# Prompt head norm moved to compression's banks, and the low half of w_out emitted ahead of the samples' value stage

## The chip, the cores and the metric

The kernel runs on one core of one Trainium2 chip. The metric is device microseconds of one execution. Before the change it takes 1236.41 us (median of 3 runs, 1235.61 to 1237.87).

## The reference

One inference step of a decoder layer, for a prompt of 512 tokens and for 8 samples of 4 tokens (32 rows), with shared weights of width 1024:

```
h = RMSNorm(x); P = h @ W_in
x += W_out [ headnorm(NSA(P_nsa)) || sigmoid(o) * headnorm(mLSTM(P_mlstm)) ]
x += CrossAttn(RMSNorm(x), memory K/V)
x += SwiGLU(RMSNorm(x))
y = RMSNorm_final(x)
```

NSA is sparse attention with three parts whose gated outputs are added: over compressed blocks (`compress`: a small two-layer network over each 32 rows of keys and of values), over selected blocks of 64 raw rows, and over a window of 512 rows. For the samples the cached rows are gathered from pages, transposed, scored against the queries, put through a softmax and multiplied with the gathered values. `headnorm` is an RMS norm over the 64 values of each head. The change concerns the prompt's NSA head norm, the samples' attention, and the first half of `W_out`.

## The kernel before, in words

All 544 tokens (512 of the prompt, 32 of the samples) lie in columns. The activations `oF` (the mixed heads' outputs) and `xT` (the residual) hold 8 blocks of 128 features by 544 columns. Products with weights are made of three matmuls, since a 32-bit operand is split into a high and a low part: `split` writes the high part on ACT (L213) and the low part on POOL or DVE (L214), and `mm3` issues `hi*hi`, `hi*lo` and `lo*hi` (L218 to L220). Columns are handled in two halves of 272: the low half holds prompt columns only, the high half the other 240 and the 32 samples. The split parts of the low half are the tiles `mh` and `ml`; weight chunks of `w_out` are `wraw`, split to `whi` and `wlo`.

Parts of the kernel are generators that yield between small steps. `weave` runs two of them alternately, `chain` one behind the other with its pace, `drain` runs one to its end. The text order that results gives each instruction a priority; a scheduler then orders the instructions of each engine by what it thinks is ready and by that priority. Each engine runs its own list in order, waiting where an operand or a buffer is not free.

The place in question is the end of the samples' attention, beside the second call of `compress`. Names there:

- `sample()`: for two groups of four samples each, score stage first: `keys` gathers are transposed on PE (L1518, tile `tp`), copied by `evac` (L206 on ACT, L208 on DVE, tile `kt`), multiplied with the queries (L1528, tile `sp`), and the exponentials are taken on ACT (L1701, tile `SS`). Then the value stage: `SS` is transposed (L1518), copied (`PTs`), and multiplied with the gathered values (L1722, tile `po`).
- `evac` puts one copy of every `flip[1]` on DVE and the others on ACT: 1 in 2 at first, 1 in 4 while `flip[1]` is 4.
- `finals_p`: the prompt's NSA outputs. L1398 multiplies the compressed part's probabilities with its values, L1401 adds them into `oF`, L1402 squares, L1407 sums over a head with a matmul against `bones`, L1408 copies back; then a logarithm (L1411), an exponential (L1412) and the scaling (L1415) make the norm.
- PSUM banks: `tp` has two, `sp` one, `po` one; `bd` has two, `xa` and `xc` one each. `bank(p)` takes the next bank of one pool, `rot(...)` the next of several in turn; `pxb` is the pair `xa`, `xc`. Compression uses `bd`, `xa`, `xc` (its lines L1216 to L1246, L1296); so does the projection `w_out`.
- `load_xT(i)` transposes a tile of the input x into `xT` (L1817), in six tiles; `fetch_x` loads those tiles by DMA.
- `early_mix`: splits the low half of `oF` into `mh` and `ml`, and fetches and transposes x. `open_late` and `finals_s` prepare the high half and the samples' final norm; `close_sample` is a last step.

Before the change `finals_p` is called inside `sample()`, behind the value stage of group 0, and `early_mix` is called after `drain(fg)`, that is, behind everything of the samples. Then come the loops over the chunks of `w_out` for the low half and the high half, and behind them the cross attention.

Of the kernel before, what the change touches and what calls it, by code (L numbers as in the profile page):

```python
# [6 lines left out]
F32 = mybir.dt.float32  # L7
# [29 lines left out]
def body(tc, I, O, stage=99, dbg=None):  # L37
    nc = tc.nc
    with ExitStack() as top:
        def pool(name, bufs=1, side="left", stack=None, space=None):  # L40
            kw = dict(name=name, bufs=bufs)
            if space is not None:
                kw["space"] = space
            else:
                kw["side"] = side
                kw["reuse_waits"] = "tile"
            return (stack or top).enter_context(tc.tile_pool(**kw))

        ptp = pool("ptp", 2, space=PSUM)
        psp = pool("psp", 1, space=PSUM)  # L50
        ppo = pool("ppo", 1, space=PSUM)
        pxa = pool("pxa", 1, space=PSUM)
        pxc = pool("pxc", 1, space=PSUM)
        pxb = [pxa, pxc]
        pbd = pool("pbd", 2, space=PSUM)

        def bank(p):
            if p is pxb:
                return rot(pxa, pxc)
            return p.tile([128, 512], F32, name=p_names[id(p)])  # L60
# [4 lines left out]
        def rot(*pools):  # L65
            key = tuple(id(p) for p in pools)
            turn[key] = turn.get(key, -1) + 1
            return bank(pools[turn[key] % len(pools)])
# [6 lines left out]
        right = {}  # L75

        def push(name, **kw):
            st = ExitStack()
            right[name] = st
            return pool(name, stack=st, **kw)  # L80

        def pop(name):
            right.pop(name).close()
# [43 lines left out]
        wp = push("wp", bufs=2, side="left")  # L127
# [182 lines left out]
        def drain(*gens):  # L310
            for g in gens:
                for _ in g:
                    pass
# [248 lines left out]
        p = bank(ptp)  # L562
# [33 lines left out]
        wp = push("wp", bufs=2, side="left")  # L596
# [147 lines left out]
        def need(x):  # L744
            while x not in done:
                yield 1
# [644 lines left out]
        def finals_p(var):  # L1391
            yield from need(("p", 1))
            var = var[:, :2048].rearrange("p (a b n) -> p a b n", a=2, b=2)
            for j in range(5):
                if j < 4:
                    acc = bank(psp)
                    for v in range(2):
                        nc.tensor.matmul(acc[64 * v:64 * v + 64], vcP[32 * j:32 * j + 32, v], PcT[32 * j:32 * j + 32, v],  # L1398
                                         start=True, stop=True)
                    oj = oF[:, j, :512]  # L1400
                    nc.vector.tensor_tensor(oj, oj, acc, op=OP.add)  # L1401
                    nc.scalar.activation(var[:, j // 2, j % 2], oj, AF.Square)  # L1402
                    yield
                if j > 0:
                    p = bank(ptp)
                    vj = var[:, (j - 1) // 2, (j - 1) % 2]
                    nc.tensor.matmul(p, bones, vj, start=True, stop=True)  # L1407
                    nc.scalar.activation(vj, p, AF.Copy)  # L1408
                if j < 4:
                    yield  # L1410
            nc.scalar.activation(var, var, AF.Ln, bias=eps_t)  # L1411
            nc.scalar.activation(var, var, AF.Exp, scale=-0.5)  # L1412
            for j in range(4):
                oj, vj = oF[:, j, :512], var[:, j // 2, j % 2]
                nc.vector.scalar_tensor_tensor(oj, oj, gh[:, j:j + 1], vj, op0=OP.mult, op1=OP.mult)  # L1415
            yield

        def sample():
            yield from need(("w", 1))
            sc = push("sc", side="right")  # L1420
# [120 lines left out]
            for g in range(2):  # L1541
# [29 lines left out]
                p = bank(ptp)  # L1571
# [15 lines left out]
            def half(name, g, hf, qs=range(4), ex=False):  # L1587
                r = []
                for q in qs:
                    t_ = cgs["free"].pop(0) if ex else sc.tile([128, 1024], F32, name="gat", bufs=8)  # L1590
                    gather(t_, name, 4 * g + q, 1 + hf)
                    r.append(t_)
                return r
# [50 lines left out]
            for g in range(2):  # L1644
# [22 lines left out]
                SS = sc.tile([128, 2080], F32, name="SS", bufs=2)  # L1667
# [39 lines left out]
            for g in range(2):  # L1707
                SS, rs = st_[g]
                if g:
                    yield from need("free")  # L1710
                    G[1, "v1"] += half("cache_v_slc", 1, 1, range(2, 4), True)
                PT_ = probs(lambda i: SS[:, 128 * i:128 * i + 128])
                yield
                po_ = bank(ppo)
                for c in range(4):
                    vg = G[g, "v0" if c < 2 else "v1"]
                    if c < 3:
                        PX = probs(lambda i: SS[:, 512 * c + 512 + 128 * i:512 * c + 640 + 128 * i])
                    for i in range(4):
                        ii = 4 * (c % 2) + i  # L1720
                        for q in range(4):
                            nc.tensor.matmul(po_[32 * q:32 * q + 32, 0:128], PT_[:, i, 32 * q:32 * q + 32],  # L1722
                                             vg[q][:, 128 * ii:128 * ii + 128], start=c == 0 and i == 0, stop=False)
                    PT_ = PX
                    if c == 0:
                        p = bank(ptp)
                        nc.tensor.transpose(p[:32, 0:128], SS[:, 2048:2080], ident)
                        PN_ = sc.tile([32, 128], F32, name="PN")
                        nc.vector.tensor_copy(PN_, p[:32, 0:128])
                    if c == 1 and g == 0:  # L1730
                        G[1, "v0"] = half("cache_v_slc", 1, 0)
                    if c == 3 and g == 0:
                        G[1, "v1"] = half("cache_v_slc", 1, 1, range(2))
                    yield
                nc.tensor.matmul(po_[:, 0:128], PN_, kvs[:, 384:512], start=False, stop=True)
                nc.vector.reciprocal(rs[:, 2:3], rs[:, 1:2])
                nc.vector.tensor_tensor(rs[:, 2:3], rs[:, 2:3], g3[:, g, 1:2], op=OP.mult)
                nc.vector.scalar_tensor_tensor(ocs[:, g], po_[:, 0:128], rs[:, 2:3], ocs[:, g], op0=OP.mult, op1=OP.add)
                yield
                if g == 0:  # L1740
                    yield from finals_p(sc.tile([128, 2080], F32, name="SS", bufs=2))
            pop("sc")
            pop("mixS")

# [30 lines left out]
        hot = {}  # L1775
# [22 lines left out]
        def fetch_x(ids, t_):  # L1798
            for i, x in zip(ids, t_):
                t0, n = xtl[i]  # L1800
                xts[i] = x
                nc.sync.dma_start(x[:n], I["x_prompt"][0, t0:t0 + n] if i < 5 else I["x_sample"].rearrange("b t d -> (b t) d"))

        def cgat():
            return cgp.tile([128, 2048], F32, name="cgat", bufs=2)

        def cgat_x():
            t_ = cgat().rearrange("p (i d) -> p i d", i=2)
            return [t_[:, 0], t_[:, 1]]

        def load_xT(i):
            t0, n = xtl[i]
            x = xts[i]
            for c in range(2):
                p = rot(psp, ppo)
                for k in range(4):
                    nc.tensor.transpose(p[:, n * k:n * k + n], x[:n, 512 * c + 128 * k:512 * c + 128 * k + 128], ident[:n, :n])  # L1817
                evac(xT[:, 4 * c:4 * c + 4, t0:t0 + n], p[:, :4 * n].rearrange("p (k t) -> p k t", k=4))

        def close_sample():  # L1820
            load_xT(5)
            yield

        def early_mix():
            hot["wp"] = push("wp", bufs=2, side="right")
            hot[0] = [wt.tile([128, KT, HALF], R32, name=f"m{c}", bufs=1) for c in "hl"]
            for k in (4, 5, 6, 7, 0, 1, 2, 3):
                split(hot[0][0][:, k], hot[0][1][:, k], oF[:, k, :HALF], nc.gpsimd if k % 2 else nc.vector)
            fetch_x((2, 3), cgat_x())
            fetch_x((4, 5), cgat_x())  # L1830
            for i in range(5):
                load_xT(i)

        def front():
# [31 lines left out]
        def wo_chunk(c):  # L1866
            return lambda: load_w([wo[:, 256 * c:256 * c + 256]], KT, fill=wo_fill(c))

        wt = hot["wt"] = push("wt", bufs=2, side="left")
# [4 lines left out]
        won.append((raw1,) + tuple(wt.tile([128, 2048], R32, name=f"w{x}").rearrange("p (k c) -> p k c", k=KT)  # L1874
                                    for x in ("hi", "lo")))
        fetch_x((0, 1), [wt.tile([128, D], F32, name=f"xt{i}", bufs=1) for i in range(2)])
        drain(fg)
        flip[1] = 2
        early_mix()
        hxp, lp, wp = hot["hx"], hot["lp"], hot["wp"]  # L1880
        if stage == 5:
            drain(finals_s())
# [9 lines left out]
        acc = [kct[:, 0, :HALF], acct[:, hs[1]]]  # L1892
# [697 lines left out]
        for hf in (1, 0):  # L2590
            for j in range(8):
                p = rot(*dbk)
# [24 lines left out]
```

## Time and profile before

| | |
|---|---|
| median of 3 runs | 1236.41 us |
| profiled execution | 1243.24 us, of which the span is 1241.5 us |
| mean granted PE clock | 0.974 |
| PE busy | 1174.3 us, 95% |
| DVE busy | 841.2 us, 68% |
| ACT busy | 612.4 us, 49% |
| POOL busy | 558.6 us, 45% |
| PE busy, 530 to 590 us | 48.42 of 60 us |

The profiled execution is 6.83 us longer than the median of the runs; its span leaves out 1.7 us around the program. Times in the text below are microseconds from the span's start. A row of the instructions in order of time gives start, length, engine, line, operation, output and inputs; a square bracket at its end gives the idle time ahead of it and what ended it.

### The profile page before, as it was taken

To read this page: it belongs to the slowest core of one execution; us is meant where nothing else is said; L and a number is where in the kernel's file an instruction comes from. 1 tells how busy PE (TensorE), PEld (TensorE's weight loads), DVE (VectorE), ACT (ScalarE), POOL (GpSimd) and SP (SyncE) were. 2 spreads that over 40 slices of the span, in tenths; PEclk is the share of its full clock that TensorE was granted. 3 is DMA by queue.
4 is the path that set the end of the run, shared out by engine and by line. 5 is a ranking of instruction groups with operands and counts; after the bars stand their busy time and mean duration, and the time that the engine had idled before them with its cause. 6 is when DMAs were issued, how large, how long until landed. Compare 5 with 4: busy or idle time off the path is not lost.

```text
span 1241.5 us, 24581 instructions
## 1 busy us (share of the span) xinstructions
PE 1174.3 (95%) x9220; PEld 1066.7 (86%) x9220; DVE 841.2 (68%) x1901; ACT 612.4 (49%) x1414; POOL 558.6 (45%) x686
## 2 busy tenths in 40 slices
PE   7999999899997989988999989999899999999996
PEld 5998999588885878854999987599899999999996
DVE  6337683567787687653754756554998888888874
ACT  5235665745545444466542423342665565555452
POOL 1013353566666266542342100043885576476342
PEclk9999999899997999999999998999999999999998
DMA  7324240141253185566767298630032333322411
GB/s 232 102 53 105 86 153 1 51 137 44 78 171 115 42 283 176 178 227 205 206 135 171 83 239 288 231 128 2 1 119 86 103 96 107 106 94 77 137 52 73
DMA packets 141769, 154.30 MB, mean 124 GB/s; under 512 B 17449, under 2 KB 123689, under 8 KB 141394
## 3 DMA queue, kind: packets, MB, share of 16 engines
q1 hardware_dynamic: 131922, 119.17, 32.0%
q0 software_dynamic: 9728, 33.56, 8.3%
q8 instruction: 73, 1.20, 0.4%
q14 instruction: 46, 0.38, 0.1%
HBM read 141.67 MB, written 13.12 MB: 125 GB/s over the span
## 4 chain that ended last, share of the span: by engine, by line
PE 49%; DVE 8%; ACT 3%; DMA 2%; issue 2%; SPq 1%; POOL 1%; POOLq 0%; DVEq 0%; ACTq 0%
PE xc L2291 7%; PE xa L2291 7%; PE bd L2291 5%; PE tp L2291 5%; PE bd L220 3%; PE bd L219 3%; PE bd L218 3%; DVE sp L2231 1%; DMA mkv<-in_cache_mem_k 1%; PE xa L1296 1%; PE tp L1518 1%; PE bd L2190 1%; PE xa L218 1%; PE xa L219 1%; PE xa L220 1%
## 5 line engine op out<-in xcount | busy, mean ns | idle before, releaser
L214 POOL TENSOR_TENSOR al<-fraw,ah 128x512 fp32r<-128x512 f32 (+1 forms) x104 | 127.5, 1227 | 152.4 <-ACT ah L213 124.0
L213 ACT ACTIVATE whi<-wraw 128x1024 fp32r<-128x1024 f32 (+3 forms) x74 | 62.5, 890 | 57.5 <-DMA wraw<-in_w_xv 28.2
L214 DVE TENSOR_TENSOR wlo<-wraw,whi 128x1024 fp32r<-128x1024 f32 (+3 forms) x74 | 73.6, 1026 | 19.1 <-ACT whi L213 19.0
L213 ACT ACTIVATE ah<-fraw 128x512 fp32r<-128x512 f32 (+1 forms) x112 | 65.8, 593 | 38.0 <-PE xc L2291 11.8
L218 PE MATMUL bd<-w1h,xh 128*128 128x256 f32 x256 | 82.6, 325 | 0.9 <-issue 0.9
L220 PE MATMUL bd<-w1h,xl 128*128 128x256 f32 x256 | 75.6, 298 | 3.0 <-DVE xl L214 3.0
L1198 POOL TENSOR_TENSOR xs<-xf 128x256 f32<-128x256 f32 x64 | 55.8, 878 | 50.2 <-PE xa L1296 30.5
L219 PE MATMUL bd<-w1l,xh 128*128 128x256 f32 x256 | 75.7, 297 | 0.0
L1296 PE MATMUL xa<-ws,xs 128*128 128x256 f32 x256 | 71.2, 400 | 2.4 <-DVE bq L1470 1.3
L625 POOL TENSOR_SCALAR sb<-sb,rs,gat 128x128 f32<-128x128 f32 (+3 forms) x64 | 46.1, 724 | 54.4 <-DVE rs L624 40.2
L213 ACT ACTIVATE xh<-xf 128x512 fp32r<-128x512 f32 x64 | 40.0, 629 | 45.5 <-DVE xf L1191 20.0
L213 ACT ACTIVATE ah<-sp 128x512 fp32r<-128x512 f32 (+1 forms) x64 | 35.5, 555 | 50.1 <-DVE sp L2231 22.8
L220 PEld LDWEIGHTS bd<-w1h,xl 128*128 128x128 f32 x256 | 48.9, 192 | 6.4 <-DVE xl L214 3.8
L1296 PEld LDWEIGHTS xa<-ws,xs 128*128 128x128 f32 x256 | 46.5, 201 | 8.5 <-issue 2.9
L218 PEld LDWEIGHTS bd<-w1h,xh 128*128 128x128 f32 x256 | 49.1, 193 | 5.0 <-issue 3.9
L214 DVE TENSOR_TENSOR xl<-xf,xh 128x512 fp32r<-128x512 f32 x64 | 47.5, 746 | 8.6 <-ACT xh L213 7.7
L219 PEld LDWEIGHTS bd<-w1l,xh 128*128 128x128 f32 x256 | 49.4, 193 | 4.5 <-issue 2.8
L219 PE MATMUL bd<-hlo,whi 128*128 128x272 f32 x176 | 52.0, 296 | 0.0
L218 PE MATMUL bd<-hhi,whi 128*128 128x272 f32 x176 | 51.7, 294 | 0.0
L1191 DVE STREAM_TRANSPOSE xf<-cgat 128x512 f32<-128x512 f32 x64 | 44.7, 703 | 10.2 <-POOL xs L1198 8.4
L220 PE MATMUL bd<-hhi,wlo 128*128 128x272 f32 x176 | 51.3, 292 | 0.0
L2231 DVE TENSOR_TENSOR sp<-fraw 128x512 f32<-128x512 f32 (+1 forms) x32 | 47.8, 1494 | 0.2
(990 smaller groups left out, 4667.9 us busy)
## 6 DMA issues: line engine op xcount, KB each, us to landing
fraw<-in_w_gate SPq DMA_DIRECT2D x11, 1024.0 KB
fraw<-in_w_up SPq DMA_DIRECT2D x11, 1024.0 KB
fraw<-in_w_down SPq DMA_DIRECT2D x24, 384.0 KB
mkv<-in_cache_mem_k SPq DMA_DIRECT2D x64, 128.0 KB
mkv<-in_cache_mem_v SPq DMA_DIRECT2D x16, 512.0 KB
wraw<-in_w_in SPq DMA_DIRECT2D x8, 512.0 KB
wraw<-in_w_xq SPq DMA_DIRECT2D x4, 1024.0 KB
wraw<-in_w_xk SPq DMA_DIRECT2D x4, 1024.0 KB
```

The source lines that it names most:

```text
L213: nc.scalar.activation(hi, src, AF.Copy)
L214: (eng or nc.gpsimd).tensor_tensor(lo, src, hi, op=OP.subtract)
L218: nc.tensor.matmul(out, ah, bh, start=first, stop=False, **kw)
L219: nc.tensor.matmul(out, ah, bl, start=False, stop=False, **kw)
L220: nc.tensor.matmul(out, al, bh, start=False, stop=last, **kw)
L625: (nc.vector, nc.gpsimd)[1].tensor_scalar(sb[:, :n], sb[:, :n], rs, gat[:, i, 3 * h + 1 + br:3 * h + 2 + br], op0=OP.mult, op1=OP.mult)
L1191: nc.vector.transpose(xf.rearrange("p a (q i) -> p q a i", q=4), gs[0].rearrange("p (q t a i) -> p t q a i", q=4, t=4, a=4)[:, t])
L1198: nc.gpsimd.tensor_tensor(xs_.rearrange("p c (v j) -> p v c j", v=2), xg[:, 0], xg[:, 1], op=OP.add)
L1296: nc.tensor.matmul(dst[2], ops[2][:, kk], w1s[t][2][:, kk], start=t == 0 and kk == 0, stop=t == 3 and kk == 1, skip_group_check=True)
L1518: nc.tensor.transpose(p[:, 128 * i:128 * i + 128], srcs(i), ident)
L2231: nc.vector.tensor_tensor(o, a, b, op=op)
L2291: nc.tensor.matmul(p[:, :HALF], w[a][:, k], x[b_][:, k], start=first and k == 0 and i == 0, stop=last and k == n - 1 and i == 2, skip_grou ...
```

## The change

The norm `finals_p` writes its sums to the banks `bd`, `xa` and `xc` (in place of `sp` and `tp`), takes the tile `ml` of the low half as scratch, and is run by `early_mix`, not by `sample()`. `early_mix` is called ahead of `drain(fg)`, so what remains of the samples' generators comes behind it in the text. x tiles 3 to 5 are loaded and transposed in `close_sample`, and x tiles 0 to 2 use the bank `sp` alone. The buffers `wp` are opened after the drain.

```
 def finals_p(var):
...
-                    acc = bank(psp)
+                    acc = rot(pbd, pxb)
...
-                    p = bank(ptp)
+                    p = rot(pbd, pxb)
...
 def sample():
...
-                if g == 0:
-                    yield from finals_p(sc.tile([128, 2080], F32, name="SS", bufs=2))
...
 def load_xT(i):
...
-                p = rot(psp, ppo)
+                p = bank(psp) if i < 3 else rot(psp, ppo)
...
 def close_sample():
-            load_xT(5)
-            yield
+            yield 6
+            fetch_x((4, 5), cgat_x())
+            for i in range(3, 6):
+                load_xT(i)
+                yield

 def early_mix():
-            hot["wp"] = push("wp", bufs=2, side="right")
+            drain(finals_p(wt.tile([128, 2176], F32, name="ml", bufs=1)))
...
-            fetch_x((4, 5), cgat_x())
-            for i in range(5):
+            for i in range(3):
                 load_xT(i)
...
         fetch_x((0, 1), [...])
+        early_mix()
         drain(fg)
         flip[1] = 2
-        early_mix()
+        hot["wp"] = push("wp", bufs=2, side="right")
```

No instruction of PE is added or taken away; two of `load_xT`'s copies go from DVE to ACT. The order of the engines' lists changes from about 530 us on.

On ACT before, at the start of group 1's value stage (`PTs` are the copies of the transposed probabilities, `SS<-SS` with 2048 columns the norm's logarithm and exponential):

```order
L1408 ACTIVATE SS<-tp 128x512
L1411 ACT_TABLE_LOAD
L1411 ACTIVATE SS<-SS,eps_t 128x2048
L206 ACTIVATE PTs<-tp 128x512 x2
L1412 ACT_TABLE_LOAD
L1412 ACTIVATE SS<-SS 128x2048
L206 ACTIVATE PTs<-tp 128x512
L213 ACTIVATE mh<-oF 128x272
```

On ACT after the change, at the norm's place in the list (`kt` are the copies of transposed keys, the scratch is now `ml`):

```order
L1408 ACTIVATE ml<-bd 128x512
L213 ACTIVATE whi<-wraw 128x1024
L213 ACTIVATE whi<-cgat 128x1024 x2
L206 ACTIVATE kt<-tp 128x512
L213 ACTIVATE whi<-wraw 128x1024
L1408 ACTIVATE ml<-xc 128x512
L206 ACTIVATE kt<-tp 128x512 x2
L1411 ACT_TABLE_LOAD
L1411 ACTIVATE ml<-ml,eps_t 128x2048
L206 ACTIVATE kt<-tp 128x512
L1412 ACT_TABLE_LOAD
L1412 ACTIVATE ml<-ml 128x2048
```

The norm's logarithm and exponential have moved from between the `PTs` copies of the value stage to between the `kt` copies of group 1's scores.

On PE before, the first matmuls of the projection (L218, into `xa`, `bd`, `xc`) stand at the end of group 1's value stage:

```order
L1722 MATMUL po<-gat,PTs 32x128 x2
L1722 MATMUL po<-cgat,PTs 32x128 x2
L1765 MATMUL tp<-ident,po_3201 128x128
L218 MATMUL xa<-mh,whi 128x272
L218 MATMUL bd<-mh,whi 128x272
L218 MATMUL xc<-mh,whi 128x272
```

On PE after the change, from the last scores of group 1 to the first value matmuls of group 0:

```order
L1518 MATMUL tp<-ident,SS 128x128 x4
L1528 MATMUL sp<-kt,Qn 32x512 x4
L1518 MATMUL tp<-ident,SS 128x128 x4
L218 MATMUL xa<-mh,whi 128x272
L218 MATMUL bd<-mh,whi 128x272
L218 MATMUL xc<-mh,whi 128x272
L218 MATMUL bd<-mh,whi 128x272
L1727 MATMUL tp<-ident,SS 32x128
L1722 MATMUL po<-gat,PTs 32x128 x12
```

The projection's first matmuls have moved ahead of the whole value stage; behind the last of these rows its groups stand in turns with L1722 and L1518.

## Prediction

> **What bounds the kernel now.** I read the page first, then the stages from 530 to 600 us, then who waits for whom there, then the rows in order of time on PE, ACT and POOL. The page's total and its chain of waits:
>
> ```profile
> PE 1174.3 (95%) x9220; PEld 1066.7 (86%) x9220; DVE 841.2 (68%) x1901; ACT 612.4 (49%) x1414; POOL 558.6 (45%) x686
> ...
> PE 49%; DVE 8%; ACT 3%; DMA 2%; issue 2%; SPq 1%; POOL 1%; POOLq 0%; DVEq 0%; ACTq 0%
> ```
>
> PE is busy 95% of the span and leads the chain, so a change is worth what it takes from PE's idle time and its slow-clock time, no more. The change keeps PE's instructions and touches one place, so the table of stages there counts (columns: stretch, its length, then busy time of PE, PEld, DVE, ACT, POOL, then the granted clock, DMA share and GB/s):
>
> ```profile
> 540.00:550.00 10.00, 7.02 (x43) 4.20 (x45) 3.52 (x11) 7.74 (x20) 4.57 (x8) 0.83 0.88 336
> 550.00:560.00 10.00, 7.51 (x60) 4.55 (x56) 7.32 (x12) 8.09 (x14) 6.49 (x7) 1.00 0.67 221
> ...
> 570.00:580.00 10.00, 8.88 (x65) 3.90 (x66) 2.65 (x7) 3.90 (x9) 3.44 (x5) 1.00 0.82 313
> 580.00:590.00 10.00, 6.33 (x131) 4.74 (x133) 3.22 (x7) 9.42 (x11) 0.72 (x2) 1.00 0.01 2
> 590.00:600.00 10.00, 10.00 (x106) 9.17 (x95) 7.41 (x21) 5.91 (x15) 5.15 (x6) 1.00 0.84 207
> ```
>
> From 590 us, when the projection w_out runs, PE is full; before that it is not, and in both holes (540 to 560, 580 to 590) ACT is the busy one. Who made PE wait from 530 to 592 us (total us, times, longest):
>
> ```profile
> PE po L1722 <- ACT PTs L206: 3.7, 2, 3.1
> PE sp L1528 <- ACT kt L206: 3.0, 2, 2.6
> PE tp L1518 <- ACT kt L206: 1.5, 2, 0.8
> PE po L1722 <- issue: 1.1, 3, 0.4
> PE tp L1518 <- ACT whi L213: 0.8, 1, 0.8
> PE po L1722 <- DVE PTs L208: 0.7, 1, 0.7
> PE tp L1623 <- ACT kt L206: 0.5, 1, 0.5
> PE tp L1518 <- DVE kt L208: 0.2, 1, 0.2
> ```
>
> This makes 11.5 us. It falls in two parts: the value stage (po, L1722) 3.7 + 1.1 + 0.7 = 5.5 us, and the score stage (tp and sp) 3.0 + 1.5 + 0.8 + 0.5 + 0.2 = 6.0 us. The rows on ACT say why the copies PE waits for come late:
>
> ```profile
> 540.86 0.72 ACT L1701 ACTIVATE SS<-SS,bs 128x512 f32<-128x512 f32 x1
> ...
> 543.69 0.58 ACT L206 ACTIVATE kt<-tp 128x512 f32<-128x512 f32 x1
> ...
> 554.04 1.06 ACT L213 ACTIVATE whi<-wraw 128x1024 fp32r<-128x1024 f32 x1
> 554.99 2.01 ACT L213 ACTIVATE whi<-cgat 128x1024 fp32r<-128x1024 f32 x2
> 556.88 0.60 ACT L206 ACTIVATE kt<-tp 128x512 f32<-128x512 f32 x1
> 557.36 1.07 ACT L213 ACTIVATE whi<-wraw 128x1024 fp32r<-128x1024 f32 x1
> 558.31 1.10 ACT L206 ACTIVATE kt<-tp 128x512 f32<-128x512 f32 x2
> ...
> 579.22 0.59 ACT L1408 ACTIVATE SS<-tp 128x512 f32<-128x512 f32 x1
> 579.82 1.28 ACT L1411 ACT_TABLE_LOAD   x1
> 581.12 2.00 ACT L1411 ACTIVATE SS<-SS,eps_t 128x2048 f32<-128x2048 f32 x1
> 583.02 1.06 ACT L206 ACTIVATE PTs<-tp 128x512 f32<-128x512 f32 x2
> 584.11 1.28 ACT L1412 ACT_TABLE_LOAD   x1
> 585.40 1.91 ACT L1412 ACTIVATE SS<-SS 128x2048 f32<-128x2048 f32 x1
> ```
>
> ACT works in order. The four exponentials L1701 hold the copy kt from 540.86 to 543.69, the four weight splits whi hold others around 555, and the prompt norm's logarithm and exponential (L1411, L1412, each with a table load) hold the copies PTs from 579.82 to 583.02 and again to 587.31. On PE this is:
>
> ```profile
> 544.32 1.66 PE L1528 MATMUL sp<-kt,Qn 128*32 128x512 f32 x8 [2.63 <-ACT kt L206]
> ...
> 558.97 0.66 PE L1518 MATMUL tp<-ident,SS 128*128 128x128 f32 x4 [0.77 <-ACT whi L213]
> ...
> 583.65 1.08 PE L1722 MATMUL po<-gat,PTs 128*32 128x128 f32 x32 [3.14 <-ACT PTs L206]
> ...
> 588.94 0.37 PE L218 MATMUL xa<-mh,whi 128*128 128x272 f32 x1
> ...
> 591.05 0.39 PE L219 MATMUL xa<-ml,whi 128*128 128x272 f32 x1
> ```
>
> The projection's first matmul is at 588.94 and its dense run starts at 591.05, behind the whole value stage. One more cost hangs on idle time, the granted clock:
>
> ```profile
> 541.25:544.66 3.41, 0.78 (x8) 0.35 (x10) 0.48 (x3) 3.41 (x11) 1.67 (x3) 1.00 1.04 414
> 544.66:548.07 3.41, 3.41 (x17) 1.84 (x10) 1.71 (x4) 1.63 (x5) 0.78 (x1) 0.50 0.85 347
> ...
> 580.20:583.60 3.40, 0.31 (x3) 0.07 (x1) 0.28 (x1) 3.39 (x4) 0.00 (x0) 1.00 0.00 0
> 583.60:587.00 3.40, 3.35 (x72) 2.62 (x73) 0.28 (x1) 3.37 (x4) 0.00 (x0) 1.00 0.00 0
> ```
>
> After a stretch with 0.78 of 3.41 us busy PE had 0.50 of its clock for 3.41 us, which costs 3.41 x 0.5 = 1.7 us. After the longer idle of 3.14 us it kept 1.00. So whether an idle of about 3 us is followed by a slow stretch depends on where it falls.
>
> **The change part by part, costed.** The prompt norm (finals_p) no longer waits for the samples' value stage of group 0; its matmuls now stand in the score stage, and the projection's low half can start inside the value stage.
>
> *Gain, value stage.* With projection matmuls between the value matmuls PE always has something ready there: the 5.5 us of po waits go (bounds 0 and 5.5; I take 5.5, since the projection keeps PE at 10.00 of 10 us from 590 on, and its first groups need only the norm and the first weight chunks, which ACT splits from 554.04 on).
>
> *Loss, score stage, the norm on ACT.* Load, L1411, load, L1412 (1.28 + 2.00 + 1.28 + 1.91 = 6.47 us) now stand between the kt copies of group 1's scores, one copy between the two and two behind. PE has in the meantime only what the two banks of tp allow. First pair: PE still has a score group (1.0), and two key transposes (0.5 each by start distance), so 2.0 us, while ACT needs 3.28 + 0.60 = 3.9: idle about 1.7. Second pair: PE has one transpose group (0.5), ACT needs 3.19 + 0.60 = 3.8: idle about 3.1. Together 4.7 us of new waits (bounds 0, if all of it lay under other work, and 6.5, all of it bare). I take 4.7 since the rows behind each copy leave nothing else for PE.
>
> *Score stage, the rest.* The waits of before mostly stay: behind the four L1701, now also two L1223, one kt (2.9); small ones at a transpose and L1246 (0.5 + 0.5); two kt behind the whi splits (1.2 + 1.5; L1408 now adds three copies of 0.59 ahead of the splits); one PTs copy (0.3). I followed these in the changed order with the durations of the rows above: 6.9 against 6.0 us, so 0.9 lost (bounds 0 and 3). The same following of the old order gives 11.7 us, beside the 11.5 measured, so its error is some tenths on a sum, if the durations stay.
>
> *Banks.* The norm's matmuls take bd, xa and xc in place of sp and tp, so they no longer queue with the score groups (one bank sp) and the transposes (two banks tp). Compression still uses xc until its last L1246, and the first L1407 into xc stands behind that one in PE's order; the others find their banks free. I cost it at nothing; if PE has to wait there, the price is one small wait like the 0.77 us in the row at 558.97.
>
> *Splits and gathers.* The low half's four POOL splits now stand ahead of four gathers of group 1's values:
>
> ```profile
> 566.79 0.94 POOL L573 DMA_INDIRECT gat<-in_cache_v_slc,gx  x1 [5.87 <-PE po L1722]
> ...
> 570.51 0.94 POOL L573 DMA_INDIRECT gat<-in_cache_v_slc,gx  x1 [0.30 <-issue]
> ...
> 589.44 2.35 POOL L214 TENSOR_TENSOR ml<-oF,mh 128x272 fp32r<-128x272 f32 x2 [9.28 <-ACT mh L213]
> ```
>
> Four splits by 2.35 / 2 are 4.7 us. The splits follow mh on ACT, so the gathers are issued about 577 to 581 instead of 567 to 571, against a use of group 1's values that was at 583.65 and comes near 587 with the projection between. That leaves one or two microseconds behind the last landing; I cost it at nothing, with an upper end of 2 us. The first weight chunks and the x tiles move with their queue; the SP queue's load of x tiles 4 and 5 still waits for the value matmuls as before, and nothing behind the low half needs them sooner.
>
> *Two evacuations from DVE to ACT* (the alternation is still one in four inside the moved part): 2 x 0.6 us on an engine at 49%, beside dense PE: nothing.
>
> *Sum.* -5.5 + 4.7 + 0.9 = +0.1 us. Slow clock: one stretch before (1.7 us). Afterwards an idle of 1.7 and one of 3.1 with only 0.5 us of work between, so some 2.3 of 3.41 us of phase give a window with no more than the 0.78 us of work that sufficed before, about 2 in 3; and one of 2.9, by the same count about 1 in 3. So one again: 0. The profiled execution (1243.24 us, 6.83 above the median of 1236.41) would take 1243.3; on the scale of the runs 1236.5 us.
>
> [...]
>
> [...]
>
> **Rivals.**
>
> *The fill works and the norm's block is hidden (faster).* PE has the four L1407 and compression's last matmuls in the score stage; if these fall under the two ACT blocks, 4.7 shrinks to about 2. With no slow window the sum is -5.5 + 2 + 0.9 - 1.7 = -4.3: 1232. Bare minimum of the loss gives -5.5 - 1.7 = -7.2: 1229. For it: ACT at 9.42 of 10 us in the hole at 580 was the only obstacle there. Against: the kt rows stand directly behind L1411 and L1412.
>
> *The idle pair starves the clock twice (slower).* Both the 2.9 us idle and the pair are followed by a slow stretch, with the norm's block bare (6.5 in place of 4.7): +0.1 + 1.8 + 1.7 = +3.6: 1240. It decides from two slow stretches between 540 and 575 us where one was. For it: 0.78 us of work sufficed for one. Against: the 3.14 us idle got none.
>
> *The change does not do what it says*: the projection stays behind the value stage because the scheduler's priorities put it there. The order of the changed kernel shows its first groups among the value matmuls, so under 1 in 50 and no time of its own.
>
> **How the numbers follow.** A measurement tells about 0.2% (2.5 us) from no change. The idle only moves: 0.45, with its own range 1234.5 (no slow stretch, 1236.5 - 1.7) to 1238.3 (two). Faster rival 0.31, slower rival 0.24. The range from 1231 to 1240 leaves out the lowest of the first and the end of the second, 2 in 10.
>
> **What would show it.** Right: po waits near zero, first L218 of the projection near 573 instead of 588.94, and new waits of tp on kt of about 1.7 and 3.1 us beside L1411 and L1412; total idle from 530 to 592 still 11 to 12 us; PE full from about 574. Wrong: those two waits under 1 us each (then faster), po waiting for the gathers, or a projection that waits for ml (then slower).

## The result and the profile after

The changed kernel is slower. It took 1250.96 us (median of 4 runs, 1247.19 to 1254.48) against 1237.14 us before: a ratio of 1.0111, 95% interval 1.0088 to 1.0134. Measured again beside other runs it was 1.0093, interval 1.0060 to 1.0125 (f1 below), so the loss is 11 to 14 us. The forecast was no change, 1236.5 us, with an upper end of 1240.

The profiled execution took 1249.71 us, with a span of 1248.0. The page's total, and the stages that answer to those of before:

```profile
PE 1177.8 (94%) x9220; PEld 1069.4 (86%) x9220; DVE 838.6 (67%) x1899; ACT 614.8 (49%) x1416; POOL 559.9 (45%) x686
```

```profile
540.00:550.00 10.00, 6.93 (x47) 4.83 (x46) 4.19 (x20) 7.32 (x19) 2.97 (x6) 0.87 0.55 208
550.00:560.00 10.00, 8.48 (x45) 4.90 (x44) 5.52 (x11) 9.87 (x18) 2.71 (x3) 0.96 0.54 186
560.00:570.00 10.00, 5.63 (x28) 2.90 (x28) 4.26 (x7) 9.94 (x12) 3.75 (x4) 0.73 0.75 219
570.00:580.00 10.00, 10.00 (x101) 6.02 (x102) 6.20 (x14) 4.05 (x12) 4.37 (x5) 0.76 0.39 156
580.00:590.00 10.00, 10.00 (x121) 8.67 (x121) 1.11 (x5) 4.94 (x12) 4.68 (x5) 1.00 0.79 242
...
615.00:620.00 5.00, 1.42 (x9) 1.20 (x8) 3.22 (x6) 3.62 (x5) 1.48 (x1) 0.91 1.02 318
620.00:625.00 5.00, 5.00 (x33) 4.81 (x33) 3.29 (x9) 2.23 (x8) 2.64 (x4) 0.75 0.80 276
```

The stage from 580 to 590, which had 6.33 us of PE work before, is full. The hole now lies at 560 to 570, where ACT is busy 9.94 of 10 us, and a second one opens at 615. The granted clock is below 1 in six of these seven stages; before, it was 0.83 in one. Who made PE wait, from 528 to 635 us:

```profile
PE tp L1518 <- ACT kt L206: 8.8, 4, 3.1
PE xc L218 <- ACT whi L213: 3.6, 1, 3.6
```

Two markers bound the place: the last start of compression's L1296, and the first matmul of the norm behind the low half (L1913 before, L1914 after, first start), by the rows of those lines in both kernels:

```profile
L1296 PE MATMUL xa<-ws,xs x256: 377/379/796, 256.7 to 531.2; 128*128 128x256 f32 x128
L1913 PE MATMUL sp<-ones_d,kcT x8: 164/183/200, 625.6 to 626.6; 128*68 128x1 f32 x8
```

```profile
L1296 PE MATMUL xa<-ws,xs x256: 377/379/796, 259.0 to 529.4; 128*128 128x256 f32 x128
L1914 PE MATMUL sp<-ones_d,kcT x8: 164/184/200, 634.6 to 635.5; 128*68 128x1 f32 x8
```

Between them lie 94.4 us before and 105.2 after: 10.8 us more. Of these, 1.8 us are only order: 14 more matmuls of the projection (its high half, 0.125 us each by the start distance of the rows) stand ahead of the second marker after the change instead of behind it. Without them the place is 9.0 us longer; the rest of the timed loss of 11 to 14 us is not located. This stretch, called the place below, repeats well: 95.1 us in a second profile of the kernel before, 105.9 in a second one of the changed kernel. The profiled executions of the kernel before took 1243.24 and 1239.58 us, above its medians (some 1234 us in the later comparisons), so whole spans aren't compared; the place and the timed ratios are.

### The profile page after: what moved, and what is told of

It is laid out like the page before. It is cut to its first block, busy times and chain, and to the rows that moved or that the text cites. A ratio compares the mean times of both kernels' runs of the same rounds, so it can differ in the third digit from the quotient of the medians.

```text
span 1248.0 us, 24588 instructions
## 1 busy us (share of the span) xinstructions
PE 1177.8 (94%) x9220; PEld 1069.4 (86%) x9220; DVE 838.6 (67%) x1899; ACT 614.8 (49%) x1416; POOL 559.9 (45%) x686
## 4 chain that ended last, share of the span: by engine, by line
PE 49%; DVE 7%; DMA 3%; ACT 3%; issue 2%; SPq 1%; POOL 1%; DVEq 0%; POOLq 0%; ACTq 0%
PE xc L2292 7%; PE xa L2292 7%; PE bd L2292 6%; PE tp L2292 5%; PE bd L218 2%; PE bd L219 2%; PE bd L220 2%; PE tp L1518 2%; PE xa L1296 2%; DMA mkv<-in_cache_mem_k 1%; PE bd L2191 1%; PE xc L218 1%; PE xc L220 1%; PE xa L218 1%; PE xc L219 1%
## 5 line engine op out<-in xcount | busy, mean ns | idle before, releaser
L218 PE MATMUL bd<-w1h,xh 128*128 128x256 f32 x256 | 81.6, 321 | 0.0
L1296 PE MATMUL xa<-ws,xs 128*128 128x256 f32 x256 | 70.5, 397 | 2.7 <-DVE ys L1332 1.3
L1296 PEld LDWEIGHTS xa<-ws,xs 128*128 128x128 f32 x256 | 45.8, 198 | 9.1 <-issue 2.4
L218 PE MATMUL bd<-hhi,whi 128*128 128x272 f32 x176 | 52.2, 297 | 0.0
L218 PEld LDWEIGHTS bd<-w1h,xh 128*128 128x128 f32 x256 | 48.7, 191 | 3.6 <-issue 2.2
L214 DVE TENSOR_TENSOR al<-sp,ah 128x512 fp32r<-128x512 f32 (+1 forms) x64 | 40.7, 637 | 9.7 <-ACT ah L213 7.8
```

The costliest lines, as they stand in the source:

```text
L214: (eng or nc.gpsimd).tensor_tensor(lo, src, hi, op=OP.subtract)
L218: nc.tensor.matmul(out, ah, bh, start=first, stop=False, **kw)
L1296: nc.tensor.matmul(dst[2], ops[2][:, kk], w1s[t][2][:, kk], start=t == 0 and kk == 0, stop=t == 3 and kk == 1, skip_group_check=True)
```

## The experiments

Ratios are to the kernel before, timed in the same job; its medians in the three jobs (e, f and g, on three chips) were 1233.74, 1233.61 and 1234.46 us. A ratio is not the quotient of the two medians: e4's medians give 1.0036. "Place" is the stretch defined above, in the profile of each. It tells the time only roughly: f2, f3, f4, g2 and g3 have places 1.6 to 3.1 us shorter than g1 and take the same time.

| kernel | median us | ratio, 95% interval | place us |
|---|---|---|---|
| f1, changed kernel again | 1244.47 | 1.0093 [1.0060, 1.0125] | 105.9 |
| e1, norm alone early | 1238.10 | 1.0038 [1.0014, 1.0062] | 99.8 |
| e2, projection alone ahead | 1244.34 | 1.0086 [1.0057, 1.0116] | 104.6 |
| e3, changed, transposes together | 1237.60 | 1.0030 [1.0004, 1.0056] | 100.9 |
| e4, changed, fourth chunk's own buffer | 1238.23 | 1.0056 [1.0030, 1.0082] | 98.1 |
| f2, e3 and e4 together | 1233.37 | 0.9998 [0.9978, 1.0018] | 93.5 |
| f3, changed, kt copies on DVE | 1233.67 | 1.0002 [0.9980, 1.0024] | 92.0 |
| f4, e3, e4 and f3 together | 1233.05 | 1.0002 [0.9980, 1.0025] | 92.8 |
| g1, kernel before again | 1234.19 | 1.0001 [0.9977, 1.0024] | 95.1 |
| g2, before, kt copies on DVE | 1233.67 | 1.0001 [0.9977, 1.0025] | 93.2 |
| g3, changed, all kt of group 1 on DVE | 1234.68 | 1.0011 [0.9992, 1.0029] | 92.4 |
| g4, g3 with e3 and e4 | 1232.51 | 0.9979 [0.9961, 0.9998] | 92.3 |

**e1, the norm alone.** Edit to the kernel before: the banks and the scratch as in the change, and

```
-                if g == 0:
-                    yield from finals_p(sc.tile([128, 2080], F32, name="SS", bufs=2))
...
+        drain(finals_p(wt.tile([128, 2176], F32, name="ml", bufs=1)))
         drain(fg)
         flip[1] = 2
         early_mix()
```

> The norm alone is moved (its banks, its scratch tile and its place ahead of the samples' remaining steps); the splits, x tiles and the projection stay behind the samples as before. Theory A, the starved score stage (waits for kt behind the norm's logarithm and exponential, and the half-clock stretches that follow): most of the 13.8 us is here, 1243 to 1248 us, with kt waits of 8 to 9 us and three or more half-clock stretches between 540 and 580 us. Theory B, the projection's interleaving (turns between kinds of matmul, weights late): this kernel is within 3 us of before, 1235 to 1240 us, since its projection still runs in one dense piece.

```profile
PE tp L1518 <- ACT kt L206: 8.7, 4, 3.0
PE sp L1815 <- ACT oF L206: 2.2, 2, 1.3
...
550.00:560.00 10.00, 7.27 (x36) 3.35 (x38) 5.84 (x7) 9.98 (x17) 0.62 (x2) 0.92 0.40 143
560.00:570.00 10.00, 6.92 (x35) 2.84 (x27) 4.99 (x9) 8.15 (x10) 4.62 (x6) 0.67 0.99 314
```

The kernel doesn't isolate the norm. The text leaves the projection behind the samples, but the scheduler moved it all the same, presumably because the norm's results are ready early: its first matmul is at 570.28, its groups stand among the value matmuls as in the changed kernel, and 12 transposes stand singly between value matmuls here too:

```profile
570.28 0.58 PE L218 MATMUL xa<-mh,whi 128*128 128x272 f32 x1
...
587.72 0.33 PE L1518 MATMUL tp<-ident,SS 128*128 128x128 f32 x1
587.98 0.41 PE L1722 MATMUL po<-gat,PTs 128*32 128x128 f32 x2
```

The kt waits and the slow clock of the score stage are here as well (waits, then two stages above), and the loss is 0.4%, about 4.7 us (1.7 to 7.7 by the interval). What this kernel lacks of the changed one is the wait for a weight chunk near 615 us and the slow stretch behind it. So it doesn't decide between theory A and theory B.

**e2, the projection alone ahead.** Edit to the changed kernel: the norm goes back into `sample()` with banks `sp` and `tp`, and the samples are advanced up to its end before `early_mix`:

```
+                    done.add("fp")
...
+        while "fp" not in done:
+            next(fg)
         early_mix()
         drain(fg)
```

> The norm stays in the samples' value stage with its old banks; the splits of the low half and the projection are emitted ahead of the samples' steps that come behind the norm. Theory A (starved score stage): no new kt waits, at most one half-clock stretch between 540 and 580 us, so 1234 to 1239 us. Theory B (interleaving costs): slower than before by 4 us or more, 1241 to 1247 us, with the projection's third or fourth weight chunk late.

It lost 0.86%, as theory B said, and weights are late here too, though on another path than the one expected. From 600 to 615 us PE doesn't wait for a chunk itself; the x tiles' transposes (L1819) and one of the samples' matmuls (L1751) wait for copies. Those on ACT stand behind weight splits, and two of these splits wait 5.09 and 2.04 us for their weights' load:

```profile
PE sp L1819 <- ACT oF L206: 3.6, 2, 2.4
PE sp L1751 <- ACT oF L206: 2.6, 1, 2.6
PE po L1819 <- DVE oF L208: 1.6, 2, 1.3
...
600.00:610.00 10.00, 4.19 (x31) 3.18 (x29) 7.28 (x10) 3.62 (x6) 0.00 (x0) 0.77 0.78 245
610.00:620.00 10.00, 8.03 (x56) 7.65 (x57) 5.32 (x17) 4.23 (x12) 4.42 (x6) 0.71 0.31 106
```

```profile
607.54 1.06 ACT L213 ACTIVATE whi<-wraw 128x1024 fp32r<-128x1024 f32 x1 [5.09 <-DMA wraw<-in_w_out]
...
610.75 1.06 ACT L213 ACTIVATE whi<-wraw 128x1024 fp32r<-128x1024 f32 x1 [2.04 <-DMA wraw<-in_w_out]
```

So emitting the projection early can cost without the early norm, but where it costs depends on the rest of the order: this kernel does not isolate a part of the changed kernel's loss either.

**e3, transposes together.** Edit to the changed kernel, in the value stage:

```
                     if c < 3:
-                        PX = probs(...)
+                        with tc.issue_after(last_v[0].ins) if last_v else ExitStack():
+                            PX = probs(...)
```

where `last_v` holds the group's last value matmul. The order on PE differs from the changed kernel's by these transposes and by a few projection matmuls that shifted among the value matmuls.

> The changed kernel, with one edit: the four transposes of a PTs tile wait for the last value matmul of the group before, so that they stand together on PE in place of alternating one by one with value matmuls (12 alternations fewer). Theory T, the turns cost PE about 0.3 us each: 3 to 4 us less than the changed kernel, 1247 to 1248 us. If a turn costs nothing beyond its matmuls: 1251 us, the same.

The time fell more than expected: 1.0030 against 1.0093, and the place from 105.9 to 100.9. The rows show the price of a turn. In the changed kernel one stretch of 64 records of value matmuls and 8 transposes in turns (its first four rows, its last two and the next instruction):

```profile
590.08 1.06 PE L1722 MATMUL po<-gat,PTs 128*32 128x128 f32 x26
591.07 0.33 PE L1518 MATMUL tp<-ident,SS 128*128 128x128 f32 x1
591.33 0.41 PE L1722 MATMUL po<-gat,PTs 128*32 128x128 f32 x2
591.67 0.33 PE L1518 MATMUL tp<-ident,SS 128*128 128x128 f32 x1
...
595.24 0.33 PE L1518 MATMUL tp<-ident,SS 128*128 128x128 f32 x1
595.50 0.86 PE L1722 MATMUL po<-gat,PTs 128*32 128x128 f32 x24
596.29 0.66 PE L1815 MATMUL sp<-ident,xt 128*128 128x128 f32 x4
```

and the same work in e3:

```profile
583.55 1.08 PE L1724 MATMUL po<-gat,PTs 128*32 128x128 f32 x32
584.56 0.66 PE L1518 MATMUL tp<-ident,SS 128*128 128x128 f32 x4
585.15 1.08 PE L1724 MATMUL po<-gat,PTs 128*32 128x128 f32 x32
586.16 0.66 PE L1518 MATMUL tp<-ident,SS 128*128 128x128 f32 x4
586.65 0.60 PE L1817 MATMUL sp<-ident,xt 128*128 128x128 f32 x4
```

6.21 us in turns (596.29 - 590.08), 3.10 together (586.65 - 583.55): 0.39 us for each of 8 transposes, so 4.7 us for the 12 that alternate. PE counts as busy all that time, which is why no view of waits shows it. Late weights are still there (xc on whi, 4.0 us), and the half-clock stretches are no fewer (six of 3.41 us, against five), so the gain is not theirs.

**e4, a buffer for the fourth chunk.** Edit to the changed kernel: the raw weights of chunk 3 are loaded into a `wraw` tile of the pool `wp`, before the projection's loop:

```
+        raw3 = wp.tile([128, 2112], F32, name="wraw", bufs=2)[:, :2048]...
+        wo_fill(3)(raw3)
```

> The changed kernel, with one edit: the raw weights of the projection's fourth chunk go to a buffer of their own (of the pool that opens when the samples are done), so their load no longer waits for the third chunk's low part. Theory W, the 3.6 us wait of PE for that chunk and the half-clock stretch behind it cost 5.3 us: 1245 to 1247 us, and no wait of xc on whi over 1 us. If that wait is made up later (the loads of the cross attention's memory bound what follows): 1250 to 1251 us although the wait is gone.

The wait of xc on whi and the slow stretch behind it are gone, the place is 98.1 us instead of 105.9, and the ratio 1.0056 instead of 1.0093: 4.6 us (0.0037 x 1234), near the 5.3 expected. The two intervals overlap, so in time this gain is not clear of the noise by itself; the vanished wait is. Of the place's 7.8 us, 1.6 are order: 13 of the 14 projection matmuls are behind the second marker again. What had made the chunk late shows in the changed kernel's chain of waits:

```profile
604.82 0.83 DVE hl L214
...
607.34 0.15 DVE wlo L214
...
608.83 0.26 SPq L1861
...
609.14 8.52 DMA wraw<-in_w_out
617.76 1.06 ACT whi L213
618.87 0.39 PE xc L218
```

The chunk's load waits for the buffer that chunk 2's low part frees; that split stands on DVE behind the high half's splits hl, and its high part can start only when chunk 0's last group, now spread over the value stage, is done at 600 us. The load takes 8.52 us, and PE has used up chunks 1 and 2 by 615 us. In e1, where chunk 0 was done at 586.6 us, chunk 2's split started at 586.66 and PE did not wait.

**f1, the changed kernel again.**

> The changed kernel unedited, on the same chip and beside the same runs of the kernel before as the three that follow. If the first comparison holds: a ratio of 1.009 to 1.013 to before. If the chip of the first comparison was the odd one: within 1.000 to 1.006, as the three other edits measured since.

1.0093: the loss is real beside f2 to f4 too.

**f2, e3 and e4 together.**

> The changed kernel with two edits together: transposes of a PTs tile kept together, and the fourth chunk's raw weights in a buffer of their own. If turns (3 to 4 us) and the late chunk (5.3 us) add: 8 to 9 us under the unedited changed kernel of this job. If both only feed the same later wait: no more than the larger one, 5 us under it.

They add: 0.9998 is 11.7 us under f1 (0.0095 x 1234), and the place falls by 12.4 us where the single edits took 5.0 and 7.8 (in f2 as in e4, 1.6 us of it by order). The kernel stands level with before although its score stage still waits (`tp` on `kt` 8.7 us, four slow stretches at 544, 558 and twice from 565, granted clock 0.83, 0.91, 0.67 and 0.91 in the stages from 540 to 580). So the two edits seem to save some time that the change had not cost; no run applies them to the kernel before.

**f3, kt copies on DVE.** Edit to the changed kernel, in `keys`, for group 1's second to fourth score column:

```
-                evac(kt_, four_t(srcs))
+                if dve:
+                    nc.vector.tensor_copy(kt_, four_t(srcs))
+                else:
+                    evac(kt_, four_t(srcs))
```

> The changed kernel with one edit: all kt copies of group 1 of the second to fourth score column go to DVE in place of the alternation, so none stands behind the norm's logarithm and exponential on ACT. Theory A (starved score stage: 8.8 us of kt waits and three extra half-clock stretches): the kt waits on ACT fall under 4 us, at most one half-clock stretch is left between 540 and 580 us, and the time is 6 to 9 us under the unedited changed kernel. If the idle is only moved behind DVE's own queue or into the next wait: within 2 us of it.

```profile
PE tp L1518 <- DVE kt L1524: 3.2, 4, 1.7
PE tp L1518 <- ACT kt L206: 2.9, 1, 2.9
...
550.00:560.00 10.00, 7.35 (x45) 3.90 (x40) 8.68 (x14) 8.12 (x10) 3.01 (x3) 1.00 0.46 159
560.00:570.00 10.00, 7.65 (x91) 4.42 (x91) 8.32 (x13) 6.00 (x8) 4.85 (x6) 0.83 0.99 285
```

The kt waits behind the norm are gone, one slow stretch is left (the stage at 0.83), and the time is 11.2 us under f1 (0.0091 x 1234), more than the 6 to 9 expected. The edit changes the order further on: PE no longer waits for the fourth chunk, and no transpose stands singly between value matmuls any more. So f3 takes away all three costs and is no measure of the starved score stage.

**f4, all three.**

> All three edits on the changed kernel: kt copies on DVE, transposes kept together, the fourth chunk's raw weights in a buffer of their own. If the three costs are separate and explain the loss: 12 to 17 us under the unedited changed kernel, so 0 to 5 us faster than before. If they overlap: between before and the best of the single edits.

Level with f2 and f3. f3's order had no single transposes and no late chunk left, so beside f3 this is no test of whether the costs overlap. Beside f2 it is one of the kt copies alone: moving them to DVE gained nothing more, and PE now waits for DVE's kt instead (3.0 us in 3 waits).

**g1, the kernel before again.**

> The kernel before, unedited, for a second profile of it: the first profiled execution of it was 6 us over its own median. If that one was typical of the place in question: 94 us from compression's last matmul L1296 to the first norm matmul behind the low half, one half-clock stretch there. If it was slow there too: 2 to 4 us less.

The place takes 95.1 us: the first profile was typical there.

**g2, the kernel before with group 1's kt copies on DVE.**

> The kernel before, with one edit: all kt copies of group 1 go to DVE. If the kt copies on ACT also cost the kernel before (2.6 us behind the exponentials, 2.3 behind the weight splits, one half-clock stretch): 4 to 6 us faster, ratio 0.995 to 0.997. If that remedy only undoes what the changed kernel added: ratio 1.000 within 0.002.

No gain: the 2.6 us wait behind the exponentials is replaced by `sp` on DVE's kt, 3.4 us in 4 waits.

**g3, the changed kernel with all kt copies of group 1 on DVE.**

> The changed kernel with all kt copies of group 1 on DVE, the first score column's four too, so the 2.9 us wait behind the four exponentials L1701 should go. If idle time there counts in full: 3 to 4 us under the version with three columns on DVE (which stood level with before), ratio 0.996 to 0.998. If the samples' chain through the softmax sets the pace there instead: level, 0.999 to 1.001.

Level with before, and no slow stretch shows (granted clock 1.00 in every stage of 10 us from 540 to 620). A place 13 us shorter than the changed kernel's thus only gives back what the change cost.

**g4, g3 with e3's and e4's edits.**

> The same with transposes kept together and the fourth chunk's raw weights in a buffer of their own. If turns still cost there (the order shows alternation of single transposes with value matmuls in group 1): 2 to 3 us under the previous kernel. If with the kt copies gone from ACT nothing of the other two costs is left: level with it.

0.9979, interval 0.9961 to 0.9998: 2.6 us faster than before by the ratio, the best of all kernels here, though its interval nearly touches 1 and it is the best of many. Against g3 it gains 3.9 us (0.0032 x 1234), more than the 2 to 3 expected, by intervals that just overlap; g3's order had nine transposes standing singly between value matmuls, which at 0.39 us are 3.5. Whether it beats the kernel before is not settled.

## Why the prediction was wrong

Point by point, with the place's 10.8 us as the account.

- *Value stage, -5.5.* Right: po no longer waits, and the first L218 of the projection starts at 573.07, forecast near 573.
- *Norm's block on ACT, +4.7, and the rest of the score stage, +0.9.* The mechanism was right, the size smaller: the kt waits sum to 8.8 us, forecast 11.6 in all, so +2.8 against 6.0 before. The wait behind the first table load (forecast 1.7) does not show, because the clock had just been halved (0.50 from 561.1 to 564.5 us, where the eight score matmuls took 1.94 us, against 1.06 at 554.92) and PE's transposes ahead of it took until the copy was ready; the one behind the second was 3.05 us (forecast 3.1). The idle from 530 to 592 us was 8.75 us, not 11 to 12.
- *Slow clock, "one again: 0".* This step failed, and it is the largest term. The profile shows five stretches of 3.41 us at 0.50 in the place, against one: at 547.4, 561.1, two from 567.9, and 619.1. Taking half of PE's occupied time in each (1.7, 1.6, 2.7 for the two, and 1.7 for the stretch behind the late chunk) gives 7.7 us by estimate, 6.0 more than before. The forecast counted a window as slow when it held no more than 0.78 us of work, the one figure that it had; that was its estimate, and no run shows such a limit. In the changed kernel windows with up to 1.77 us of work were followed by half clock (the rows stand further down in this section). The idles of 1.5 and 1.3 us behind the weight splits, which it had listed but not counted for the clock, went with a slow stretch of their own (0.50 from 561.1 us), and the late chunk's 3.6 us with one more (0.50 from 619.1).
- *"The first weight chunks and the x tiles move with their queue ... nothing behind the low half needs them sooner."* This step failed too. The low half itself needs the fourth chunk, its load hangs on a chain through ACT, DVE and SP that starts only when the first chunk is used up, and here that was at 600 us, which left too little work to cover the load of 8.52 us: 3.6 us of wait.
- *"A change is worth what it takes from PE's idle time and its slow-clock time, no more."* This failed as well: turns between kinds of matmul are not in the sum. The same matmuls were priced by their rows in dense runs; in the new order 12 transposes alternate one by one with value matmuls at 0.39 us each.
- *The account:* -5.5 + 2.8 + 6.0 + 3.6 = 6.9; 14 projection matmuls more stand ahead of the second marker by the orders, 14 x 0.125 = 1.8; the remaining 2.1 is left for the turns. That is less than the 4.7 of e3's rows. The kernel before has no such turns, but one of its groups of 32 records of value matmuls, broken up by the three "issue" waits near 571 us, occupies PE for 2.0 us beside the waits, where most groups take 1.0. The other 1.6 us was not followed.
- *Slips in the sum:* the low end of its middle case should be 1236.5 - 1.7 = 1234.8, not 1234.5, and its two waits are 3.28 + 0.60 - 2.0 = 1.9 and 3.19 + 0.60 - 0.5 = 3.3 as written, not 1.7 and 3.1. Neither changes the outcome.

The rival that ended slower had the right sign and one of the three mechanisms: it named two slow stretches and the norm's block, and gave 1240; the weights and the turns were in no rival. Experiments and rows together settle that the turns cost time (e3 against f1 and f2 against e4, by intervals that don't overlap, though on different chips), that the late chunk is a second cost (its wait goes with e4's edit), and that without these two the kernel is level (f2). What the slow clock of the score stage costs is worked out from the trace alone: no experiment changes it and nothing else. What the norm's place costs by itself stays open, since e1 brought the turns with it.

The slow stretches of the changed kernel in the place start whole multiples of 3.41 us apart (547.45, 561.10, 567.93, 571.34 and 619.13), so the stretches ahead of them can be laid on the same grid; PE was busy for a part of each:

```profile
557.69:561.10 3.41, 0.84 (x6) 0.42 (x4) 3.41 (x4) 3.41 (x6) 0.00 (x0) 1.00 0.00 0
561.10:564.51 3.41, 3.20 (x14) 1.21 (x15) 0.95 (x2) 3.38 (x4) 0.94 (x1) 0.50 0.60 193
564.51:567.93 3.42, 1.77 (x12) 1.09 (x11) 1.10 (x3) 3.39 (x4) 2.05 (x3) 1.00 0.97 271
567.93:571.34 3.41, 1.95 (x12) 0.92 (x12) 2.45 (x4) 2.98 (x6) 0.77 (x1) 0.50 1.06 347
571.34:574.75 3.41, 3.41 (x25) 2.07 (x21) 3.19 (x7) 1.00 (x3) 2.70 (x4) 0.50 0.72 285
```

The other two held 1.22 us (544.03 to 547.45) and 0.27 us (615.71 to 619.13). On such a grid, laid on its slow stretch at 544.66, the kernel before's idle of 3.14 us falls across two windows with 1.72 and 1.97 us of work (from 578.79 and 582.21), and neither was followed by half clock. So PE's busy time in the window ahead does not tell by itself whether half clock follows; over the changed kernel's whole span, on its own grid, a window with 2.21 us of work (from 247.08) was followed by it and one with 1.46 us (from 8.14) was not. In the windows from 557.69 and 564.51 PE's work was transposes alone (L1518); whether the kind of work matters was not tested.

The table loads on ACT took the 1.28 us that the forecast had counted (at 561.76 and 565.65), and ACT was idle for 0.02 us ahead of the first and for 0.02 us behind it:

```profile
560.63 1.11 ACT L206 ACTIVATE kt<-tp 128x512 f32<-128x512 f32 x2
561.76 1.28 ACT L1411 ACT_TABLE_LOAD   x1
563.06 2.00 ACT L1411 ACTIVATE ml<-ml,eps_t 128x2048 f32<-128x2048 f32 x1
```

## What to carry to other kernels

When ready work is moved into another stage to fill its waits, ask what that work was covering where it stood: here it hid weight loads, and a wait of 3.6 us for one opened at 615 us, some 40 us behind the first moved matmul. Look at the order of an edited kernel before calling it one half of a change: in e1 moving the norm alone moved the projection too. Price the order and not only the instructions: here single transposes between small matmuls doubled the time of the two together (6.21 us against 3.10) while PE counted as busy. And several waits of 1 to 3 us close together cost more here than their sum: beside 8.8 us of kt waits the score stage had four stretches of 3.41 us at 0.50 of the clock, 6.0 us by the estimate above (1.7, 1.6 and 2.7).

## What was not expected of the hardware

A 128x128 transpose standing singly between value matmuls (stationary operand of 32 columns) cost 0.39 us more than the same transpose beside others (6.21 against 3.10 us for 64 value records and 8 transposes). And in the 3.41 us windows ahead of a halved clock PE was still busy up to 1.77 us at full clock in the changed kernel's place, against 0.78 us in the one window that the forecast had.
